# An RWKV-7 scan by quarters of its heads, its steps set between the products of the next quarter, and all late modulation sums on TensorE's column strips

## The chip, the cores and the metric

The kernel runs on one core of a Trainium2 chip. The metric is the time of one execution on the device in microseconds. Three runs of the kernel before gave 2135.18, 2140.97 and 2140.46 us; the median is 2140.46 us.

## The reference

Two blocks follow each other on one sequence of T = 256 tokens with D = 2048 channels, everything in float32. The change touches the first block's mixer and the modulation:

```python
mod = silu(c) @ ada_w + ada_b                  # six rows of 2048, from one vector c
sh_m, sc_m, g_m, sh_f, sc_f, g_f = split(mod + ada_table)
h = rms(x) * (1 + sc_m) + sh_m
r, k, v = (h + xx * mu[i]) @ w_rkv[i]          # each 2048 x 2048
# decay, a, g from low-rank products; kk = normalised k
def step(state, inp):                          # 32 heads of 64, over 256 tokens
    sa = state @ a_t
    state = state * w_t + sa b_t' + v_t k_t'
    return state, state @ r_t
y = groupnorm(y) * ln_w + ln_b + sum(r * k * r_k) * v
y = (y * g) @ w_o
x = x + g_m * rms(y)
h = rms(x) * (1 + sc_f) + sh_f
x = x + g_f * rms(conv_ffn(h))                 # then the second block
```

The scan is computed by chunks of 64 tokens. Inside a chunk of a head one 64x64 triangular system has to be inverted; from chunk to chunk the 64x64 state of the head is carried, so the four chunks of a head run in order, while heads are independent of each other.

## The kernel before

Every float32 weight tile of 128x1024 is read into a buffer "raw", split by ScalarE (ACT) into a high part "whi" (L142) and by VectorE (DVE) into the rest "wlo" (L146), and multiplied in three products on TensorE (PE): high by high, high by low, low by high. `fm_unit` (L149 to L159) does it with the tokens as the moving columns, 128x256 a product, 48 products for a weight tile pair of 2048 rows and 128 columns; `tm_units` (L161 to L192) does it with 512 weight columns moving. `split` (L133 to L147) is their common front.

The stages around the change are these, in time of the profiled execution. Until about 306 us the kernel makes the early modulation, v, k and the low-rank hidden layers. **The r stage**, about 306 to 467 us, is a loop over the 16 pairs of heads (L551 to L628): for each pair j it makes two low-rank products, the decay (L576 to L586, with tanh and exp on ACT), the r product (48 products of `fm_unit`) and the operands AR, BK and EC of the scan, which for all 16 pairs stay on the chip. The instruction at L605 is the first that reads the r product of a pair. **The scan**, 467 to 730 us, runs over all heads: `diag_gram` (L642) makes the products of 32x32 diagonal blocks, a mask and a transposition; `invert_diag` (L663) inverts 32 blocks at a time on 128 partitions in 30 dependent steps, each a product L680 and an addition L683 on DVE, in two column ranges (`PARTS`), and is run twice, for two chunks at a time; `gram`, `bt_make` and `invert_off` make the rest of the chunk's matrices. Then `chunk` (L746) runs four times. In it a group of 4 pairs goes through three steps: `stage_r` (products, then two copies to SBUF by ACT at L762), `stage_u` (products with these copies, two copies by ACT at L775), and `stage_o` (output and state products, state update on DVE at L801 to L804). The four groups of a chunk are independent and take turns, and `norm` (L824) of finished groups, the inversion for the later chunks, the gram products of the next chunk and the projection `e_proj` (L869) are set between them. **The w_o stage** follows from 698.7 us on in part and runs alone to 820.3 us; then the residual is added and the FFN's input made (the handover).

**The late modulation sums** are the twelve groups of 512 columns that the later rows g_m, sc_f and sh_f need. Before the change `ada_group` (L221 to L250) makes them on DVE: 16 row blocks of 128x512 for a group, each multiplied by a column of silu(c) and added to an accumulator (L239 for the first of a group, L245 for the others). One step of the generator is two reads of 512 KB and four blocks. The tables `RSKIP`, `ASTEP`, `OSTEP` and `LATE` set how many steps stand in the r stage, the scan, the w_o stage and the handover. The early sums use `ada_group_pe` instead (L252 to L268): four column strips of 32 columns of PE, block b on strip b mod 4, the weights as 512 moving columns (L263).

The program is written in this order, and the builder places each engine's instructions by its own estimate of when their inputs are ready, so that pieces of different loops stand between each other. Each engine then runs its own list in order. All reads and writes named here are issued by SyncE (SP), in the order of its list.

Of the kernel before, what the change touches and what calls it, by code (L numbers as in the profile page):

```python
# [8 lines left out]
F32 = mybir.dt.float32  # L9
# [7 lines left out]
NRAW, NRAW2 = 4, 5  # L17
NADA = 5
NADA2 = 3
NGL, NSTEP = 2, 2  # L20
HEAD = "d0 e v0 g0 b0 d1 g1 b1 e i0 e".split()
EPOS = ((0, 4),)
XL = 4
VST, WST, WP = (2, 2, 2, 2), (0, 0, 0, 0), 2
WLEAD = 5
EARLY = (("NT", 2), ("NT", 2), ("XT", 2), ("XT", 2))
# [4 lines left out]
A01 = (0, 1) * 6  # L31
ASTEP = (A01, A01, (0, 1, 1, 0, 1, 1, 0, 1, 1, 0, 1, 1), (1, 1, 1, 1, 1, 1, 0, 0))
OSTEP = (2, 2, 2, 0)
RSKIP = (0, 4)
# [31 lines left out]
def body(tc, A, out):  # L66
# [277 lines left out]
    sil32 = t_(pa, [P, KT, 32], "sil32")  # L344
# [42 lines left out]
    ada_how[0] = ada_group  # L387
# [95 lines left out]
    ada_how[0] = ada_group  # L483
# [47 lines left out]
    wide_m[0] = True  # L531
    pha.close()


    adx = ExitStack()
    adap[0] = adx.enter_context(pool("adap2", NADA2, side="right"))
    accp[0] = adx.enter_context(pool("accp", 2, side="right"))
    phb = ExitStack()
    pb = phb.enter_context(pool("pb", 1, side="right", reuse_waits="tile"))
    AR = t_(pb, [P, NPAIR, 4, P], "AR")  # L540
    BK = t_(pb, [P, NPAIR, 4, P], "BK")
    EC = t_(pb, [P, NPAIR, 4], "EC")
# [3 lines left out]
    bd = drm.tile([NPAIR, P, T], F32, tag="bd", name="bd")  # L546

# [6 lines left out]
    for j in range(NPAIR):  # L554
# [3 lines left out]
        l2h = t_(pr, [P, 4, P], "l2h", F32R, bufs=2)  # L558
        l2l = t_(pr, [P, 4, P], "l2l", F32R, bufs=2)
# [12 lines left out]
        for q, nm in ((0, "w"), (1, "a")):  # L572
            z = ps("m")
# [3 lines left out]
            th.append(t1)  # L577
        S.activation(th[0], th[0], AF.Copy, bias=1.0)
# [7 lines left out]
        S.activation(EC[:, j, :], c3(pc)[:, :, 63], AF.Exp, scale=C1)  # L586
# [5 lines left out]
        rb = ps("m")  # L592
# [3 lines left out]
        ar, bk = AR[:, j], BK[:, j]  # L596
# [12 lines left out]
        bb = ps("m")  # L609
# [6 lines left out]
        vT = t_(pr, [P, T], "vT", bufs=2)  # L616
        S.activation(vT, tp[:, :T], AF.Copy)
        V.tensor_tensor(vT, vT, bb[:, :T], op=ALU.mult)
        z = ps("s")
        low_rank(z[:, :T], [(2, "g0"), (3, "g1")])  # L620
        V.scalar_tensor_tensor(vT, vT, vcol(V_LNB, j), z[:, :T], op0=ALU.add, op1=ALU.mult)
        SP.dma_start(bd[j], vT)
        gs = t_(pr, [P, T], "gs", bufs=2)
        S.activation(gs, z[:, :T], AF.Copy, scale=vcol(V_LNW, j))
        SP.dma_start(gd[j], gs)
        if j % 8 not in RSKIP:
            next(ada, None)

    phr.close()
    whl_x.close()  # L630
    lora.close()


    phs = ExitStack()
    pc_ = phs.enter_context(pool("scan", 1, reuse_waits="tile"))
    ST = t_(pc_, [P, NPAIR, P], "ST")
    G.memset(ST, 0.0)
    yd = drm.tile([P, NPAIR, 2, 64], F32, tag="yd", name="yd")
    GT, UVs, NTs, XTs = {}, {}, {}, {}
    dmask = cst[:, DMK:DMK + 32]  # L640

    def diag_gram(w):  # L642

        a4 = t_(pc_, [P, 32, 32], "TQ")
        gp = [ps("s"), ps("s")]
        for e in range(2):
            for b in range(2):
                os_ = slice(e * 64 + b * 32, e * 64 + b * 32 + 32)
                bs = slice(b * 32, b * 32 + 32)
                for i in range(NPAIR):  # L650
                    for hd in range(2):
                        hs = slice(hd * 64, hd * 64 + 64)
                        mm(gp[hd][os_, i * 32:i * 32 + 32], BK[hs, i, 2 * w + e, bs], AR[hs, i, 2 * w + e, bs],
                           start=True, stop=True)
        ah = a4.rearrange("p (i h) t -> p i h t", h=2)
# [838 lines left out]
```

## Time and profile before

| | |
|---|---|
| median of three runs | 2140.46 us (2135.18 to 2140.97) |
| the profiled execution | 2133.21 us, span of the trace 2131.4 us |
| PE busy | 1979.3 us, 93% |
| DVE busy | 1385.3 us, 65% |
| ACT busy | 972.3 us, 46% |
| moved by DMA | 445.25 MB, mean 209 GB/s |

The profile is one execution. "Busy" counts an engine's instructions; matmuls are pipelined, so a matmul's own duration is longer than the interval to the next one. The granted clock is TensorE's, in tenths of full speed on the page and as a fraction in a window. An entry such as "idle 5.3 <-DVE wlo L146 5.3" says that the engine stood still for 5.3 us in all before this group of instructions, and that the end of a DVE instruction of line 146 on the tile wlo ended it.

### The profile page before, as it was taken

The page shows a single profiled execution, that of the slowest core. Times are in us where ns is not written, and L with a number is a line of the kernel's source. Part 1 is how long each engine was busy: PE and PEld are TensorE (multiplying, and loading weights), DVE is VectorE, ACT ScalarE, POOL GpSimd, SP SyncE. Part 2 cuts the span into 40 slices and gives each one's busy share as a digit, 9 for nine tenths or more (in the row PEclk, how much of TensorE's full clock was granted, in tenths as well). Part 3 has the DMA queues.
Part 4 walks back from the last instruction along what each step waited for, and adds up shares of the span by engine and source line. Part 5 has one row for each costly group of instructions (what it writes and reads, how often), then busy time and mean ns, then how long its engine had stood idle before and what let it go on. Part 6 is the DMA issues. An engine that isn't in the chain of part 4 may idle for free.

```text
span 2131.4 us, 36666 instructions
## 1 busy us (share of the span) xinstructions
PE 1979.3 (93%) x14708; PEld 1735.8 (81%) x14708; DVE 1385.3 (65%) x2203; ACT 972.3 (46%) x1514; POOL 386.8 (18%) x193
## 2 busy tenths in 40 slices
PE   6999989988878697899999999999989999999998
PEld 3688868886667486899999999788867899998887
DVE  3687899879778878966676766333353655656435
ACT  3544465533323244455545455344445444444453
POOL 1000000010000001323223232223232222222232
PEclk8999999998778798999999999999999999999999
DMA  8888668863667797866675766665645445456564
GB/s 279 309 273 299 208 223 293 259 182 108 151 159 214 233 324 256 278 224 191 194 251 190 213 202 196 217 192 188 195 153 170 134 166 164 159 163 208 184 201 148
DMA packets 189035, 445.25 MB, mean 209 GB/s; under 512 B 40120, under 2 KB 62776, under 8 KB 187328
## 3 DMA queue, kind: packets, MB, share of 16 engines
q1 hardware_dynamic: 188864, 442.91, 64.9%
q8 instruction: 115, 1.88, 0.4%
q14 instruction: 56, 0.46, 0.1%
HBM read 427.10 MB, written 15.75 MB: 208 GB/s over the span
## 4 chain that ended last, share of the span: by engine, by line
PE 63%; DVE 8%; DMA 6%; issue 1%; ACT 1%; SPq 0%; POOL 0%; DVEq 0%; ACTq 0%; POOLq 0%
PE ps_s L157 6%; PE ps_s L159 6%; PE ps_s L158 6%; PE ps_g L159 4%; PE ps_g L157 4%; PE ps_g L158 4%; PE ps_g L174 4%; PE ps_g L172 4%; DMA raw<-in_ada_w 4%; PE ps_g L173 4%; PE ps_s L172 4%; PE ps_s L174 4%; PE ps_s L173 4%; DVE acc L245 2%; DVE wlo L146 1%
## 5 line engine op out<-in xcount | busy, mean ns | idle before, releaser
L142 ACT ACTIVATE whi<-raw 128x1024 fp32r<-128x1024 f32 x558 | 590.1, 1059 | 665.6 <-PE ps_g L173 139.8
L146 DVE TENSOR_TENSOR wlo<-raw,whi 128x1024 fp32r<-128x1024 f32 x410 | 504.1, 1232 | 411.8 <-ACT whi L142 409.2
L146 POOL TENSOR_TENSOR wlo<-raw,whi 128x1024 fp32r<-128x1024 f32 x148 | 363.9, 2460 | 1085.7 <-ACT whi L142 1046.7
L159 PE MATMUL ps_g<-xh,wlo 128*128 128x256 f32 x816 | 233.8, 287 | 5.3 <-DVE wlo L146 5.3
L159 PE MATMUL ps_s<-xh,wlo 128*128 128x256 f32 x816 | 228.1, 279 | 7.3 <-DVE wlo L146 5.7
L157 PE MATMUL ps_g<-xh,whi 128*128 128x256 f32 x816 | 232.5, 285 | 0.5 <-ACT whi L142 0.5
L158 PE MATMUL ps_g<-xl,whi 128*128 128x256 f32 x816 | 231.4, 284 | 0.0
L157 PE MATMUL ps_s<-xh,whi 128*128 128x256 f32 x816 | 227.6, 279 | 0.0
L158 PE MATMUL ps_s<-xl,whi 128*128 128x256 f32 x816 | 227.4, 279 | 0.0
L245 DVE SCALAR_TENSOR_TENSOR acc<-raw,sil,acc 128x512 f32<-128x512 f32 x240 | 200.4, 836 | 35.3 <-DMA raw<-in_ada_w 33.6
L159 PEld LDWEIGHTS ps_g<-xh,wlo 128*128 128x128 f32 x816 | 158.0, 194 | 10.0 <-DVE wlo L146 7.5
L159 PEld LDWEIGHTS ps_s<-xh,wlo 128*128 128x128 f32 x816 | 155.0, 190 | 8.4 <-DVE wlo L146 6.5
L157 PEld LDWEIGHTS ps_g<-xh,whi 128*128 128x128 f32 x816 | 158.2, 194 | 2.7 <-issue 1.9
L158 PEld LDWEIGHTS ps_g<-xl,whi 128*128 128x128 f32 x816 | 158.0, 194 | 0.6 <-issue 0.3
L158 PEld LDWEIGHTS ps_s<-xl,whi 128*128 128x128 f32 x816 | 155.2, 190 | 0.0
L157 PEld LDWEIGHTS ps_s<-xh,whi 128*128 128x128 f32 x816 | 155.1, 190 | 0.0
L157 PE MATMUL ps_s<-h3h,whi 128*128 128x256 f32 x384 | 109.7, 286 | 0.0
L159 PE MATMUL ps_s<-h3h,wlo 128*128 128x256 f32 x384 | 108.4, 282 | 0.0
L158 PE MATMUL ps_s<-h3l,whi 128*128 128x256 f32 x384 | 108.2, 282 | 0.0
L582 POOL MEMSET ep<- 128x4 f32 x16 | 1.7, 107 | 437.9 <-DVE AR L605 225.1
L157 PEld LDWEIGHTS ps_s<-h3h,whi 128*128 128x128 f32 x384 | 72.4, 189 | 3.6 <-issue 3.5
L157 PE MATMUL ps_g<-h3h,whi 128*128 128x256 f32 x256 | 74.3, 290 | 0.0
(509 smaller groups left out, 4637.1 us busy)
## 6 DMA issues: line engine op xcount, KB each, us to landing
raw<-in_w_f SPq DMA_DIRECT2D x258, 512.0 KB, 4.6
raw<-in_ada_w SPq DMA_DIRECT2D x192, 512.0 KB, 5.3
raw<-in_w_i2f SPq DMA_DIRECT2D x80, 512.0 KB, 3.7
raw<-in_w_o SPq DMA_DIRECT2D x60, 512.0 KB, 5.1
raw<-in_w_v SPq DMA_DIRECT2D x32, 512.0 KB, 4.5
raw<-in_w_k SPq DMA_DIRECT2D x32, 512.0 KB, 5.1
raw<-in_w_r SPq DMA_DIRECT2D x32, 512.0 KB, 5.7
raw<-in_w_g SPq DMA_DIRECT2D x32, 512.0 KB, 4.8
```

The costliest lines, as they stand in the source:

```text
L142: S.activation(hi, raw, AF.Copy)
L146: e.tensor_sub(lo, raw, hi)
L157: mm(acc, wh[:, sl], xh[:, kt, :], start=(kt == 0), stop=False)
L158: mm(acc, wh[:, sl], xl[:, kt, :], start=False, stop=False)
L159: mm(acc, wl[:, sl], xh[:, kt, :], start=False, stop=(kt == KT - 1))
L172: mm(a, xh, wh[:, sl], start=st, stop=False)
L173: mm(a, xl, wh[:, sl], start=False, stop=False)
L174: mm(a, xh, wl[:, sl], start=False, stop=sp_)
L245: V.scalar_tensor_tensor(acc, raw[:, a, :], sc, acc, op0=ALU.mult, op1=ALU.add)
L582: G.memset(ep[:, :, 0:1], 1.0)
```

## The change

There are three parts.

First, the scan is cut by heads instead of by chunks alone. A quarter is 4 pairs, that is 8 heads. `scan(q)` does for a quarter all that was done for all heads: 32 diagonal blocks (8 heads by 4 chunks) on 64 partitions, one inversion of 30 steps, the gram products and transpositions between its steps, and four chunks whose three steps now have no other group beside them. The r stage of a pair has become the generator `operands`, with three points at which it hands over. At each of them, three steps of the scan of the quarter before are run (`SSTEP`). The scan of the last quarter has no later quarter: its steps stand beside the projection e, the reading back of the first three quarters' results from `yd`, and the first w_o products. Operands AR, BK and EC are held for two quarters instead of for all pairs.

Second, all late modulation sums use `ada_group_pe`, one step at each of the 48 hand-over points of the r stage (`QSTEP`); none stands in the w_o stage or the handover. The 192 instructions of L239 and L245 that they took on DVE go, 192 matmuls of 512 columns on strips come. The reads are the same, and there are three buffers for them (`NADA2`), as before.

Third, what this needs in space: two instead of three buffers for the split weights in the r stage (`NWHL`), one buffer for some operands that had two, and no early reading of w_o (`EARLY`, `WLEAD`).

The core of the diff:

```diff
-NRAW, NRAW2 = 4, 5
+NRAW, NRAW2, NWHL = 4, 5, 2
+SSTEP, QSTEP = 3, 1
-ASTEP = (A01, A01, (0, 1, 1, 0, 1, 1, 0, 1, 1, 0, 1, 1), (1, 1, 1, 1, 1, 1, 0, 0))
-OSTEP = (2, 2, 2, 0)
-RSKIP = (0, 4)
...
-    ada_how[0] = ada_group
     ada = ada_run(ADALAG, *[ada_row(2, k0, 4, V_NMP, gmd) for k0 in range(0, KT, 4)],
...
+    whl_x.close()
+    whl[0] = whl_x.enter_context(pool("whlr", NWHL, reuse_waits="tile"))
     adap[0] = adx.enter_context(pool("adap2", NADA2, side="right"))
...
-    for j in range(NPAIR):
+    def operands(j, AR, BK, EC):
...
         V.tensor_tensor(bk[:, :, 64:128], c3(k2), em, op=ALU.mult)
+        yield
         racc = ps("g")
         fm_unit(A["w_r"][j], xr, racc[:, :T])
+        yield
         rr = racc[:, :T]
...
         SP.dma_start(bd[j], vT)
-        if j % 8 not in RSKIP:
-            next(ada, None)
+        yield
...
+    def scan(q, AR, BK, EC):
         a4 = t_(pc_, [P, 32, 32], "TQ")
+        gp = [ps("m"), ps("m")]
+        for c in range(4):
             for b in range(2):
+                for i in range(4):
                     for hd in range(2):
+                        mm(gp[hd][bs, o:o + 32], BK[hs, i, c, bs], AR[hs, i, c, bs], start=True, stop=True)
+        ah = a4[0:64].rearrange("p (x h) t -> p x h t", h=2)
...
+        NT = t_(pc_, [P, 32, 32], "NT")[0:64]
+        V.transpose(NT, a4[0:64].rearrange("p u t -> p t u"))
+        yield
...
         for jj in range(30, 0, -1):
...
+            for c0, c1, n, pv in td:
+                V.tensor_tensor(pv, XT[:, c0:c1, jj:jj + 1].broadcast_to([64, n, jj]),
+                                NT[:, jj:jj + 1, 0:jj].broadcast_to([64, n, jj]), op=ALU.mult)
+            for c0, c1, n, pv in td:
                 V.tensor_tensor(XT[:, c0:c1, 0:jj], XT[:, c0:c1, 0:jj], pv, op=ALU.add)
+            if jj % 3 == 0:
+                next(sd, None)
+                yield
...
+        for c in range(4):
...
+            for hd in range(2):
                 S.activation(rs[:, hd, :], rp[hd * 64:hd * 64 + 64, 0:256], AF.Copy)
+            behind()
+            yield
             up = ps("s")
...
+            for hs in hss:
+                S.activation(uv[0:64, :, hs], up[hs, 0:256].rearrange("p (i d) -> p i d", d=64), AF.Copy)
+            behind()
+            yield
+            oy = ps("g" if q < 3 else "m")
...
+            S.activation(ys, oy[:, 256:].rearrange("p (i t) -> p i t", t=64), AF.Copy)
+            todo.append(norm(q, c, ys, gl, bl))
+            behind()
             yield
...
+    sc = iter(())
+    for q in range(4):
+        AR = t_(pb, [P, 4, 4, P], "AR")
+        BK = t_(pb, [P, 4, 4, P], "BK")
+        EC = t_(pb, [P, 4, 4], "EC")
+        for i in range(4):
+            for _ in operands(q * 4 + i, AR, BK, EC):
+                for _ in range(SSTEP):
+                    next(sc, None)
+                for _ in range(QSTEP):
+                    next(ada, None)
+        for _ in sc:
             pass
+        sc = scan(q, AR, BK, EC)
+    for _ in ada:
+        pass
...
+    for e, _ in enumerate(sc):
+        if e % 3 == 0:
+            nb = next(ep_, None)
+            if nb is not None:
+                e_proj(nb, pT)
+        elif e % 3 == 1:
+            q = next(yq, None)
+            if q is not None:
...
+                SP.dma_start(yt, yd[:, q4, :])
+                for hf in range(2):
+                    y_split(yh[hf][:, :, q4, :], yt[:, :, hf * P:hf * P + P])
...
-                 [(nb, kt, kt == 0, kt == KT - 1) for kt in range(KT)], lead=WLEAD if nb == 0 else 0, more=more, tail=TAIL if nb == 3 else 0,
-                 early=early if nb == 0 else ())
+                 [(nb, kt, kt == 0, kt == KT - 1) for kt in range(KT)], tail=TAIL if nb == 3 else 0)
...
-        for _ in range(OSTEP[nb]):
-            next(ada, None)
```

The order of PE in a chunk. Before, the products of one chunk step (L755 is `stage_r`, L772 `stage_u`, L786 and L788 `stage_o`) stand beside those of another group and the projection e (L869):

```order
L869 MATMUL ps_g<-raw,ys 128x512 x2
L755 MATMUL ps_s<-uv,xh 64x64
L772 MATMUL ps_s<-rs,xh 64x64 x8
L869 MATMUL ps_g<-raw,ys 128x512 x2
L786 MATMUL ps_g<-uv,BK 64x64 x2
L788 MATMUL ps_g<-xh,uv 64x64 x2
```

After, L150 to L152 are the three r products of the next quarter (L157 to L159 before), L613 is another product of the r stage, L784, L797 and L808 to L813 are the steps r, u and o of a chunk, and L665 is a norm's last product:

```order
L152 MATMUL ps_g<-xh,wlo 128x256
L150 MATMUL ps_g<-xh,whi 128x256
L151 MATMUL ps_g<-xl,whi 128x256
L152 MATMUL ps_g<-xh,wlo 128x256
L797 MATMUL ps_s<-rs,GT 64x64 x8
L665 MATMUL ps_m<-rx,selc 128x256
L784 MATMUL ps_s<-uv,GT 64x64 x2
L613 MATMUL ps_s<-qb,cst 128x256
L808 MATMUL ps_g<-uv,BK 64x64 x2
L810 MATMUL ps_g<-GT,uv 64x64 x2
L813 MATMUL ps_g<-AR,ST 64x64 x2
L808 MATMUL ps_g<-uv,BK 64x64 x2
```

Between two steps of one quarter's chunk there now stand products of the next quarter's r stage and a norm, and no other group of heads.

The order of PE in the r product. Before, it is a plain run of three alternating products, with low-rank products (L567 to L569) between:

```order
L569 MATMUL ps_a<-lhiw,l2l 128x256
L159 MATMUL ps_g<-xh,wlo 128x256
L157 MATMUL ps_g<-xh,whi 128x256
L158 MATMUL ps_g<-xl,whi 128x256
L159 MATMUL ps_g<-xh,wlo 128x256
```

After, matmuls on strips (L256, which was L263) stand between them, in groups of changing length:

```order
L594 MATMUL ps_s<-rk_146,selc 128x256
L256 MATMUL ps_a<-raw,sil_102 32x512 x2
L150 MATMUL ps_g<-xh,whi 128x256
L151 MATMUL ps_g<-xl,whi 128x256
L256 MATMUL ps_a<-raw,sil_102 32x512 x10
L152 MATMUL ps_g<-xh,wlo 128x256
L150 MATMUL ps_g<-xh,whi 128x256
```

In the r stage after the change there are 70 such groups with 192 matmuls: 18 groups of one, 26 of two, 5 of three, 11 of four, 5 of five, 3 of six and 2 of ten.

The order of ACT around the norm's square root. Before, one table load (at L336) stands at the first norm, and the copies of the chunks (L762, L775) need none:

```order
L762 ACTIVATE rs<-ps_s 64x256 x2
L793 ACTIVATE ys<-ps_g 128x256
L775 ACTIVATE uv<-ps_s 64x4x64 x2
L835 ACTIVATE rt<-ps_m 128x256
L336 ACT_TABLE_LOAD
L336 ACTIVATE rn<-ps_m,epsr 8x64
L871 ACTIVATE gl<-ps_g 128x512
L762 ACTIVATE rs<-ps_s 64x256
```

After, L655 is the norm's square, L329 its square root, and L586 an exponential of the r stage:

```order
L575 ACTIVATE zs<-ps_s 128x256
L584 ACTIVATE ep<-pc 128x4x64
L577 ACTIVATE gs<-zs,vec 128x256
L329 ACT_TABLE_LOAD
L329 ACTIVATE rn<-ps_m,epsr 8x64
L586 ACT_TABLE_LOAD
L586 ACTIVATE em<-pc 128x256
L587 ACTIVATE EC<-pc 128x4
```

The square roots of the norms and the exponentials and tanhs of the r stage now alternate on ACT: the whole program has 25 table loads after the change and 11 before, and 13 of the 25 lie in the r stage with the scans beside it and in the last scan.

## Rows read from the trace of the kernel before

**Rows 1.** The page: granted TensorE clock in tenths, and GB/s, in 40 slices.
```profile
PEclk8999999998778798999999999999999999999999
...
GB/s 279 309 273 299 208 223 293 259 182 108 151 159 214 233 324 256 278 224 191 194 251 190 213 202 196 217 192 188 195 153 170 134 166 164 159 163 208 184 201 148
```

**Rows 2.** Windows by stage: length, engines' busy time (instructions), granted clock, DMA share, GB/s.
```profile
306.00:318.00 12.00, 11.34 (x81) 10.46 (x81) 11.37 (x17) 8.03 (x16) 0.00 (x0) 0.93 0.84 286
318.00:467.00 149.00, 140.18 (x1031) 128.94 (x1030) 135.12 (x259) 82.91 (x176) 3.91 (x17) 0.94 0.80 248
467.00:730.00 263.00, 205.36 (x2929) 162.28 (x2922) 206.57 (x514) 78.26 (x182) 6.96 (x6) 0.77 0.65 175
730.00:821.00 91.00, 90.03 (x388) 73.54 (x388) 70.81 (x87) 35.63 (x46) 1.74 (x1) 0.98 0.84 296
821.00:846.00 25.00, 10.19 (x70) 9.50 (x71) 21.03 (x38) 13.78 (x34) 6.38 (x3) 0.66 0.60 222
```

**Rows 3.** One source line (L605, the r product's first reader), with first and last start.
```profile
L605 DVE TENSOR_TENSOR AR<-ps_g,ep x16: 413/424/426, 318.1 to 466.5; 128x256 f32<-128x256 f32 x16
```

**Rows 4.** Timeline of PE in a weight tile's products: start, duration, operation.
```profile
437.52 0.28 PE L159 MATMUL ps_g<-xh,wlo 128*128 128x256 f32 x1
...
440.40 0.28 PE L159 MATMUL ps_g<-xh,wlo 128*128 128x256 f32 x1
```

**Rows 5.** Timeline of PE around sums on strips (L263), two records a matmul.
```profile
39.94 1.06 PE L263 MATMUL ps_a<-raw,sil 128*32 128x512 f32 x8
...
43.92 1.05 PE L263 MATMUL ps_a<-raw,sil 128*32 128x512 f32 x2
...
44.90 0.50 PE L425 MATMUL ps_s<-wlo,xl 128*128 128x512 f32 x1
...
154.01 1.92 PE L263 MATMUL ps_a<-raw,sil 128*32 128x512 f32 x16
```

**Rows 6.** Lines of DVE, 306 to 822 us: instructions, busy us, mean ns, idle before.
```profile
L245 DVE SCALAR_TENSOR_TENSOR acc<-raw,sil,acc 128x512 f32<-128x512 f32 x180 | 135.0, 751 | 26.1 <-DMA raw<-in_ada_w 24.9
...
L680 DVE TENSOR_TENSOR pt<-XT,NT 128x108 f32<-128x108 f32 (+33 forms) x106 | 22.6, 247 | 0.1
...
L683 DVE TENSOR_TENSOR XT<-XT,pt 128x108 f32<-128x108 f32 (+33 forms) x106 | 22.4, 246 | 0.1
...
L723 DVE STREAM_TRANSPOSE TQ<-XT 32x1024 f32<-32x1024 f32 x4 | 7.9, 1966 | 0.0
...
L803 DVE TENSOR_TENSOR ST<-ST,ps_g 64x256 f32<-64x256 f32 x16 | 6.6, 415 | 0.3
```

**Rows 7.** Lines of ACT, 306 to 822 us.
```profile
L775 ACT ACTIVATE uv<-ps_s 64x256 f32<-64x256 f32 x32 | 12.1, 379 | 6.8 <-PE ps_s L772 6.4
...
L762 ACT ACTIVATE rs<-ps_s 64x256 f32<-64x256 f32 x32 | 12.1, 379 | 20.3 <-PE ps_s L759 15.6 <-remote 3.2 <-PE ps_s L755 0.5
...
L336 ACT ACT_TABLE_LOAD x1 | 1.3, 1283 | 0.0
```

**Rows 8.** Timeline of ACT around a table load.
```profile
312.65 1.28 ACT L576 ACT_TABLE_LOAD   x1
313.95 0.48 ACT L576 ACTIVATE thw<-ps_m,dv 128x256 f32<-128x256 f32 x1
```

**Rows 9.** Lines of PE, 460 to 730 us.
```profile
L869 PE MATMUL ps_g<-raw,ys 128*128 128x512 f32 x32 | 20.3, 794 | 0.0
```

**Rows 10.** One source line (L172, w_o's first product), with first and last start.
```profile
L172 PE MATMUL ps_g<-whi,xh x32: 392/392/628, 698.7 to 795.2; 128*128 128x512 f32 x32
...
L172 PE MATMUL ps_s<-whi,xl x32: 388/390/392, 754.7 to 819.5; 128*128 128x512 f32 x32
```

**Rows 11.** Timeline of DVE at the handover.
```profile
818.90 0.75 DVE L245 SCALAR_TENSOR_TENSOR acc<-raw,sil,acc 128x512 f32<-128x512 f32 x1 [0.73 <-DMA raw<-in_ada_w]
...
819.69 2.74 DVE L245 SCALAR_TENSOR_TENSOR acc<-raw,sil,acc 128x512 f32<-128x512 f32 x1
```

**Rows 12.** The page: DMA issues, KB each, us to landing.
```profile
raw<-in_ada_w SPq DMA_DIRECT2D x192, 512.0 KB, 5.3
```

More of the change, by code (lines that the diff above doesn't have):

```diff
@@ new lines, in scan, with uv_load, side @@
+        yield
+        Gt = t_(pc_, [P, 32, P], "GT")
+        g4 = Gt.rearrange("p (c i h) t -> p c i h t", i=4, h=2)
+        def uv_load(c):
+            uv = t_(pc_, [P, 4, P], "uv", bufs=2)
+            SP.dma_start(uv[64:128].rearrange("p i d -> p (i d)"),
+                         vd[c // 2, (c % 2) * 64:(c % 2) * 64 + 64, q * 512:(q + 1) * 512])
+            G.memset(uv[0:64], 0.0)
+            return uv
+        def side():
+            for c in range(4):
+                gram(g4, c, AR, BK)
+                yield
+            for c in range(3):
+                bt_make(c, BK)
+                yield
@@ L743, in invert_off, with behind @@
         yield
-    def chunk(c, ys):
-        Gt, uv = GT[c], UVs[c]
-        def stage_r(i4):
+        ST = t_(pc_, [P, 4, P], "ST")
+        G.memset(ST, 0.0)
+        todo = []
+        def behind():
+            while todo:
+                try:
+                    next(todo[0])
+                    return
+                except StopIteration:
+                    todo.pop(0)
+        hss = [slice(hd * 64, hd * 64 + 64) for hd in range(2)]
+        for c in range(4):
+            un = uv_load(c + 1) if c < 3 else None
+            cs = slice(c * 64, c * 64 + 64)
+            gl = t_(pc_, [P, 4, 64], "gl", bufs=2)
+            SP.dma_start(gl, gd.rearrange("j p t -> p j t")[:, q * 4:q * 4 + 4, cs])
+            bl = t_(pc_, [P, 4, 64], "bl", bufs=2)
+            SP.dma_start(bl, bd.rearrange("j p t -> p j t")[:, q * 4:q * 4 + 4, cs])
@@ L766, in stage_u @@
+            yield
             up = ps("s")
             for i in range(4):
[L768 removed]
                 o = slice(i * 64, i * 64 + 64)
[L770 to L775 removed]
@@ L873, in e_proj @@
             S.activation(ev[:, 512:1024], ev[:, 0:512], AF.Square, accum_out=esq[:, hf, nb:nb + 1])
-    def run(*gs):
-        for _ in chain(*gs):
-            pass
-    EP = iter(range(4))
-    def dgg(w):
-        diag_gram(w)
-        yield
-    def epg():
-        nb = next(EP, None)
-        if nb is not None:
-            e_proj(nb)
-        yield
-    HD = {"d0": lambda: dgg(0), "d1": lambda: dgg(1), "v0": lambda: invert_diag(0, PARTS), "i0": lambda: invert_off(0),
-          "i1": lambda: invert_off(1),
-          "g0": lambda: gram(0), "g1": lambda: gram(1), "b0": lambda: bt_make(0), "b1": lambda: bt_make(1), "e": epg}
@@ L1047, in body @@
     accs = tm_accs()
-    wx = ExitStack()
-    more = wx.enter_context(pool("wx", WLEAD - 3, side="right", reuse_waits="tile")) if WLEAD > 3 else None
     for nb in range(4):
```

357 lines of the change are left out of this document (115 added, 242 removed).

## The prediction

> **What bounds the kernel now.** I read the page's clock and GB/s lines first, to see where the engines are not fed [rows 1]: from the tenth to the fourteenth slice the clock digits are 7 and 8 and the DMA moves 108 to 233 GB/s, while the fifteenth, in w_o, reaches 324. The windows by stage give the reason for each stage [rows 2]. In the r stage PE is busy 140.18 of 149 us and DVE 135.12: both are nearly full, at a granted clock of 0.94. In the scan PE has 205.36 and DVE 206.57 of 263 us, at a clock of 0.77: neither is full, they wait for each other, and PE works slower because of it. The w_o stage is PE alone, 90.03 of 91 us at 0.98. At the handover DVE is busy 21.03 of 25 us. One pair of heads takes (466.5 - 318.1)/15 = 9.9 us in the r stage [rows 3]; its 48 r products have an interval of (440.40 - 437.52)/24 = 0.12 us, so 5.8 us of it [rows 4]. From 306 us to the end of w_o's last product at about 820.3 us (the last L172 starts at 819.5 [rows 10] and two products follow) it is 514 us, and this stretch is what the change rebuilds. DVE is busy in it for 135.12 + 206.57 + 70.81 = 412 us, of which 135.0 are the late sums [rows 6]: 180 instructions of 751 ns.
>
> **The change, part by part.** I add up the new stretch as four pieces, all against the profiled execution.
>
> A. The first quarter has no scan beside it. Each pair now reads 1 MB of w_r, about 0.77 MB of small operands and stored rows, and three steps of two reads of 512 KB for the late sums, together 4.98 MB (before, 12 steps stood over 16 pairs). The fastest slice of the trace moves 324 GB/s, the r stage 248 and w_o 296 [rows 1, 2]. At 324 a pair takes 15.4 us, at 296 16.8, where it took 9.9. Since some of the sums' data is read ahead I take 15, that is 60 us for four pairs, and the 12 us from 306 to the first L605 as before: 72. Bounds: 66 (reads well ahead) and 80 (at 296 and an SP list that stands behind a full buffer). PE's work, 37 + 18 us by the figures of B, lies under it.
>
> B. Three quarters with a scan beside them. For each:
> r products and operands: PE is busy 140.18/149 of the 9.9 us, 9.3 us a pair, 37 us. DVE's relief does not lower this, since PE is nearly full there already.
> Sums on strips: four matmuls on four strips take 1.06 us, one alone takes the same (1.05, and PE's next product starts 0.98 after it), eight take 1.92 [rows 5]. So a group costs about 0.96 us for each four or part of four. The 70 groups of the order are 82 such turns, 79 us in all, about 20 us a quarter. Bounds: at the rate of eight, 0.24 a matmul, 48 of them are 11.5 us; each alone at 0.98 is 47. The order decides for the middle.
> Scan on PE: 205.36 less the 20.3 of projection e [rows 9] is 185 us at a clock of 0.77. At 0.98 this would be 145, so 36 to 46 a quarter; I take 37, since r products keep PE busier than the scan alone did.
> Hand-overs: before, four groups of a chunk took turns, and an ACT copy of one lay beside another's products. Now a quarter has one group, and its steps r, u and o follow each other through two pairs of ACT copies of 379 ns [rows 7] and four state updates of 415 ns on DVE [rows 6]: 4 x 0.379 + 4 x 0.415 = 3.2 us a chunk, 12.7 for four. r products stand between them in the order, but not after every step. Between 0 (all covered) and 12.7 I take 8.
> Table loads: 13 of 1.283 us [rows 7, 8] lie in this stretch, four a quarter, 5 us of ACT; ACT is busy 82.91 of 149 us in the r stage, so most of it is hidden. Bounds 0 and 5, I take 2.
> In the trace the activation after such a load starts 0.02 us after its end [rows 8], so a load costs its 1.283 us and nothing more. The Trainium skill (ScalarE: Activation LUTs, section What ACT_TABLE_LOAD costs) adds a drain of about 1380 ns for every switch, 2.66 us; by that rule, four would be 11 us of ACT a quarter and, with the same share hidden, the sum would be 2 us a quarter higher. The trace doesn't show the drain.
> Together 37 + 20 + 37 + 8 + 2 = 104 a quarter, 312 for three. DVE has 135 us less to do, but 32 blocks on 64 partitions are inverted four times instead of twice: L680 and L683 take 22.6 + 22.4 = 45 us for two [rows 6], so 22.5 for each quarter and 45 more in all. That leaves DVE at 412 - 135 + 45 = 322 us of the new stretch: not the bound, except while an inversion runs. By a rule of the Trainium skill (TensorEngine Tiling (Array Packing), section Key Properties), a change of the tiling mode drains TensorE; the strips force two for every group. Beside it the trace has PE's next product 0.98 us after a single strip matmul [rows 5], which is in my price already.
>
> C. The scan of the last quarter alone. It is a chain, and only projection e (20.3 us, rows 9) and the first w_o products fill it: inversion 22.5; transpositions of 1.97 us [rows 6], four of them, 8; four chunks at 3.2 us of copies and updates plus three runs of small products and their hand-overs, estimated 8.5 each, 34; the diagonal products, gram masks, off blocks, last norm and split have no row in which they lie alone, estimated 30 (15 to 45). Sum 95, from 80 to 110.
>
> D. What is left of w_o. Of 384 products the order has 133 beside the last scan, 251 behind it, at 90.03/388 = 0.232 us [rows 2]: 58.
>
> 72 + 312 + 95 + 58 = 537 against 514: 23 us later. At the handover, DVE's late sums go, the last of which run from 819.69 for 2.74 us, past PE's end [rows 11]: 3 back. The FFN's four groups stay as they are. So 20 us longer: 2133.2 becomes 2153, and as the profiled execution lies 7.3 us under the median, the forecast is 2160 us.
>
> **The rivals.**
> First, faster: the products cover every hand-over, and PE keeps the upper of its two levels (1.2 and 2.4 GHz) through the scans, as in w_o (0.98), where the old scan had 0.77 [rows 2]. Then a quarter is 35 of r stage, 14 of strips, 36 of scan, 3 of the rest, 88; A 70, C 88 and D 58: 480, which is 34 less, and 3 at the handover: 2103. For it speaks that PE waits for DVE in the old scan and that 135 us of DVE work go; against it that the strips put new work on PE, which is the fuller engine in the r stage and in w_o. It decides as soon as a quarter takes less than about 97.
> Second, slower still: the strips stand in PE's list ahead of r products, and their data comes through three buffers, each landing 5.3 us after its issue [rows 12]. A group of ten matmuls needs five reads, two more than there are buffers. If each of a quarter's 12 steps of two reads waits 0.8 us, a quarter is 10 us longer: three make 30, 2190. Old L245 waited so, 26.1 us for 180 [rows 6], but there DVE stood, not PE.
> Third, no change: the hand-overs are covered, but the strips are not cheaper: 98 a quarter, C 90, sum 514, 2140.
>
> **How the numbers follow.** I give 0.43 to the forecast, 0.28 to the first rival, 0.17 to the second and 0.12 to the third. A measurement of this kernel can tell 0.3%, 6.4 us, from no change. The third case is the middle of "same", and the edges of its neighbours reach into it: faster 0.31, same 0.14, slower 0.55. With A from 66 to 80, C from 80 to 110 and a quarter between 96 and 112, the likeliest case's own range is 2140 to 2180; the whole one reaches to 2095, past the first rival, and up to 2198, past the second.
>
> **What would show it.** In the profile after: the windows of the first quarter's four pairs with DMA above 300 GB/s and 15 us a pair (A); 104 us between the first r products of successive quarters, the clock above 0.9, and PE idle behind the ACT copies rs and uv (B); groups of strips at about 1 us for up to four matmuls; a stretch of some 95 us with PE half idle ahead of the bulk of w_o (C). If the quarters with a scan take 90 us and PE shows no gaps there, the first rival is right and my strips and hand-overs are overpriced. If PE's waits are for the reads of ada_w, it is the second. If the first quarter takes 40 us, A fails, and the time is 20 us lower.

## The result, and the profile after

The change made the kernel slower: 2211.24 us in the median of four runs (2202.98 to 2219.71) against 2140.72, a ratio of 1.0334 with a 95% interval of 1.0286 to 1.0382, some 71 us. The forecast was 20 us slower, so the sign was right, the size was not, and 2211 lies above the range.

The page after has these two lines, the granted clock in tenths and the GB/s of 40 slices, which answer to [rows 1]:

```profile
PEclk8999998889999989899999999999999999999999
...
GB/s 291 297 297 283 206 199 205 200 200 217 197 209 152 207 150 303 212 193 180 185 183 248 181 213 190 175 233 193 191 196 135 177 144 175 170 165 219 191 197 153
```

The clock no longer falls to 7 in the old scan's slices, and the DMA moves about 200 GB/s where the r stage had 248. The windows after, in order: three pairs of the first quarter, the three quarters with a scan beside them, the start and the rest of the last scan, the bare w_o, the handover. Each quarter ends at the first reader of its last r product (L608, which was L605). The columns are those of [rows 2]: length, busy time of PE, PEld, DVE, ACT and POOL with instructions, granted clock, DMA share, GB/s.

```profile
323.20:384.00 60.80, 44.99 (x288) 30.33 (x287) 22.96 (x46) 18.54 (x40) 0.32 (x3) 0.89 0.72 223
384.00:511.40 127.40, 104.60 (x1094) 73.18 (x1098) 76.38 (x212) 47.62 (x97) 3.56 (x11) 0.88 0.76 203
511.40:620.90 109.50, 104.76 (x1104) 71.80 (x1100) 75.69 (x214) 45.56 (x95) 3.13 (x10) 0.97 0.66 202
620.90:730.10 109.20, 104.43 (x1104) 71.03 (x1100) 75.19 (x212) 43.78 (x92) 3.13 (x10) 0.97 0.58 177
730.10:770.30 40.20, 31.32 (x273) 16.40 (x268) 27.78 (x100) 16.34 (x32) 0.15 (x1) 0.96 0.77 220
770.30:831.00 60.70, 55.75 (x608) 40.82 (x608) 37.95 (x80) 25.49 (x50) 1.04 (x2) 0.89 0.47 145
831.00:899.30 68.30, 66.65 (x290) 53.68 (x288) 50.52 (x61) 29.10 (x38) 1.46 (x1) 1.00 0.90 313
899.30:925.00 25.70, 10.05 (x63) 9.24 (x63) 23.27 (x41) 16.33 (x39) 6.63 (x3) 0.67 0.61 209
```

Against the terms of the sum: A was 72 us and is 384.0 - 306 = 78. B was 104 a quarter and is 127.4, 109.5 and 109.2, together 346 instead of 312. C was 95 and is 101. D was 58 and is 68.3, since 98 products of w_o were run beside the last scan, not 133. Together 593 us, where the sum had 537: the stretch ends at 899.4 us instead of 820.3, 79 later. What follows this stretch took 1302 us in this execution against 1311 before; in the runs below it took 1306 to 1320, so the 9 us are taken as the scatter of one execution and not as the change's.

In A the DMA moved 223 GB/s over the last three pairs, not above 300. These pairs took 14.3, 30.9 and 15.6 us. In the long one, a read of w_r stands in the chain that ended last (start, us, what); over the whole program such a read landed 7.3 us after its issue in the median, and 5.7 before:

```profile
345.38 13.48 DMA raw<-in_w_r
```

The first reader of the r product, with its first and last start, stretches over 407 us instead of 148 [rows 3]:

```profile
L608 DVE TENSOR_TENSOR AR<-ps_g,ep x16: 411/424/425, 323.2 to 730.1; 128x256 f32<-128x256 f32 x16
```

The strips by themselves, PE's busy time on L256 in the first two quarters with a scan, some 48 matmuls of two records each:

```profile
384.00:511.40 127.40, 23.82 (x100) 3.25 (x104) 0.88 0.76 203
511.40:620.90 109.50, 25.84 (x100) 3.75 (x96) 0.97 0.66 202
```

Their price of 20 us was 24 to 26. What PE waited for in the same two quarters (total us, times, longest):

```profile
PE ps_a L256 <- DMA raw<-in_ada_w: 15.3, 3, 9.0
...
PE ps_a L256 <- DMA raw<-in_ada_w: 2.4, 3, 1.6
```

So in the first of them PE stands 15.3 us for reads of the late sums, and in the second hardly at all; there PE is busy 104.76 of 109.5 us at a clock of 0.97. The chain that ended last, within each of the two quarters by lines (the view ends the row where it does), says the same: 21.7% and 4.0% of it are these reads.

```profile
by line: DMA raw<-in_ada_w 21.7%; PE ps_a L256 13.4%; PE ps_g L152 7.7%; PE ps_g L150 7.4%; PE ps_g L151 7.1%; another core or an unknown queue 3.6%; PE ps_m L636 2.4%; PE ps_s L561 1.9%; DVE wlo L139 1.9%; PE ps_m L653 1.9%; PE ps_m L665 1
...
by line: PE ps_a L256 18.4%; PE ps_g L151 5.9%; PE ps_g L150 5.7%; PE ps_g L152 5.4%; PE ps_m L636 5.2%; DMA raw<-in_ada_w 4.0%; PE ps_s L561 3.3%; PE ps_g L808 2.8%; PE ps_m L665 2.8%; PE ps_m L273 2.5%; PE ps_g L810 2.4%; PE ps_s L613 2.3
```

Read alone, the second quarter says that PE is the bound and the strips are the loss. The experiments show that this is not all of it.

DVE's inversion, which answers to L680 and L683 of [rows 6], doubled as forecast, to 89.5 us:

```profile
L729 DVE TENSOR_TENSOR XT<-XT,pt 64x140 f32<-64x140 f32 (+28 forms) x212 | 44.8, 243 | 0.1
L726 DVE TENSOR_TENSOR pt<-XT,NT 64x140 f32<-64x140 f32 (+29 forms) x212 | 44.7, 242 | 0.1
```

The table loads cost what [rows 8] had, with the next activation 0.02 us behind:

```profile
505.27 1.28 ACT L586 ACT_TABLE_LOAD   x1
506.57 0.42 ACT L586 ACTIVATE em<-pc 128x256 f32<-128x256 f32 x1
```

At the handover nothing was won, against the 3 us of the forecast: PE waits 14.65 us for its first product (14.49 before), and the first sums of the FFN's own groups (L238) now stand where the others went.

```profile
897.37 3.54 DVE L238 SCALAR_TENSOR_TENSOR acc<-raw,sil,acc 128x512 f32<-128x512 f32 x2 [1.28 <-DMA raw<-in_ada_w]
...
914.09 0.48 PE L933 MATMUL ps_a<-cst,y 128*128 128x128 f32 x1 [14.65 <-DVE y L929]
```

### The profile page after: what moved, and what is told of

Read it like the earlier page. It is cut to its first block, busy times and chain, and to the rows that moved or that the text cites. A ratio compares the mean times of both kernels' runs of the same rounds, so it can differ in the third digit from the quotient of the medians.

```text
span 2201.2 us, 37566 instructions
## 1 busy us (share of the span) xinstructions
PE 2054.0 (93%) x15092; PEld 1728.1 (79%) x15092; DVE 1312.3 (60%) x2229; ACT 1001.7 (46%) x1554; POOL 387.7 (18%) x210
## 4 chain that ended last, share of the span: by engine, by line
PE 81%; DMA 8%; DVE 6%; ACT 3%; issue 1%; SPq 0%; another core or an unknown queue 0%; POOL 0%; ACTq 0%; DVEq 0%; POOLq 0%
PE ps_s L150 6%; PE ps_s L152 6%; PE ps_s L151 6%; PE ps_g L150 5%; PE ps_g L152 5%; PE ps_g L151 5%; PE ps_a L256 4%; DMA raw<-in_ada_w 4%; PE ps_s L165 4%; PE ps_g L167 4%; PE ps_s L166 4%; PE ps_s L167 4%; PE ps_g L166 4%; PE ps_g L165 4%; DVE wlo L139 1%; PE ps_s L438 1%
## 5 line engine op out<-in xcount | busy, mean ns | idle before, releaser
L139 DVE TENSOR_TENSOR wlo<-raw,whi 128x1024 fp32r<-128x1024 f32 x414 | 509.7, 1233 | 457.0 <-ACT whi L135 454.2
L150 PE MATMUL ps_g<-xh,whi 128*128 128x256 f32 x816 | 236.8, 290 | 14.7 <-ACT whi L135 14.7
L152 PE MATMUL ps_g<-xh,wlo 128*128 128x256 f32 x816 | 236.8, 290 | 3.0 <-DVE wlo L139 2.9
L151 PE MATMUL ps_g<-xl,whi 128*128 128x256 f32 x816 | 236.0, 289 | 0.0
L152 PE MATMUL ps_s<-xh,wlo 128*128 128x256 f32 x816 | 231.1, 283 | 2.7 <-DVE wlo L139 2.7
L150 PE MATMUL ps_s<-xh,whi 128*128 128x256 f32 x816 | 231.1, 283 | 0.0
L150 PEld LDWEIGHTS ps_g<-xh,whi 128*128 128x128 f32 x816 | 160.5, 197 | 26.3 <-ACT whi L135 16.7
L256 PE MATMUL ps_a<-raw,sil 128*32 128x512 f32 (+1 forms) x704 | 139.7, 591 | 36.5 <-DMA raw<-in_ada_w 26.6
L152 PEld LDWEIGHTS ps_g<-xh,wlo 128*128 128x128 f32 x816 | 160.2, 196 | 13.0 <-issue 6.2
L152 PEld LDWEIGHTS ps_s<-xh,wlo 128*128 128x128 f32 x816 | 156.6, 192 | 3.1 <-DVE wlo L139 3.1
L150 PEld LDWEIGHTS ps_s<-xh,whi 128*128 128x128 f32 x816 | 156.8, 192 | 0.0
L150 PE MATMUL ps_s<-h3h,whi 128*128 128x256 f32 x384 | 107.8, 281 | 0.0
L152 PE MATMUL ps_s<-h3h,wlo 128*128 128x256 f32 x384 | 106.6, 278 | 0.0
L256 PEld LDWEIGHTS ps_a<-raw,sil 128*32 128x32 f32 x704 | 23.3, 110 | 82.2 <-DMA raw<-in_ada_w 41.1
L150 PEld LDWEIGHTS ps_s<-h3h,whi 128*128 128x128 f32 x384 | 72.2, 188 | 3.6 <-issue 3.5
L152 PEld LDWEIGHTS ps_s<-h3h,wlo 128*128 128x128 f32 x384 | 72.3, 188 | 0.3 <-issue 0.3
```

Of the source, the lines that this page charges most:

```text
L139: e.tensor_sub(lo, raw, hi)
L150: mm(acc, wh[:, sl], xh[:, kt, :], start=(kt == 0), stop=False)
L151: mm(acc, wh[:, sl], xl[:, kt, :], start=False, stop=False)
L152: mm(acc, wl[:, sl], xh[:, kt, :], start=False, stop=(kt == KT - 1))
L256: mm(acc[r:r + 32, :w_], sil32[:, b, :], raw[:, a, :], start=(b < 4), stop=(b >= KT - 4))
```

## The experiments

Each is compared with the kernel before, run on the same chip in turns; the ratio is what counts. The changed kernel itself has 1.0334. The letters of the theories are those of the expectations and not the terms A to D of the sum.

**The strips without their time.**

```diff
-                mm(acc[r:r + 32, :w_], sil32[:, b, :], raw[:, a, :], start=...
+                cw = 32 if seg >= 2 else w_
+                mm(acc[r:r + 32, :cw], sil32[:, b, :], raw[:, a, :cw], start=...
```

Expected: 

> The changed kernel, but each late strip matmul moves 32 of its 512 columns (the rest of the late sums is left out); all reads of 512 KB stay. Theory A, the strips' time on TensorE is the loss: the strips go from 98 us of PE to under 15, a quarter with a scan beside it from 109 to about 88 us, the first quarter stays at its reads, the whole is 2125 to 2150 us. Theory B, the reads behind three buffers are the loss: nothing but the matmul goes, the time stays above 2190. Theory C, the cut of the scan itself is the loss (twice the inversions, one group a chunk): also above 2180, with PE waiting for DVE and ACT instead.

Measured: 1.0252 (1.0207 to 1.0298), 2204.64 us. The window of the second quarter with a scan:

```profile
505.60:609.70 104.10, 90.88 (x1105) 76.48 (x1102) 75.95 (x215) 46.06 (x94) 3.56 (x11) 0.87 0.75 227
```

The quarter went from 109.5 to 104.1 us only, with PE now at a clock of 0.87 where it had 0.97; the quarters beside it took 122.4 and 109.9 us (127.4 and 109.2 in the changed kernel). Theory A fell: the strips' time alone is not what a quarter lasts. The first quarter, with all its reads, stayed at 77.2 us.

**The sums back on DVE, in the new places.**

```diff
+    ada_how[0] = ada_group
     ada = ada_run(ADALAG, *[ada_row(2, ...
...
-        kr = t_(pr, [P, T], "kr", bufs=2)
+        kr = t_(pr, [P, T], "kr")                # and so for vl
```

Expected: 

> The changed kernel with the late sums back on DVE at the same 48 places (two one-buffer tiles in the r stage pay for the accumulators). DVE then has 75 + 36 = 111 us of work in a quarter of 109, PE 82. Theory A: a quarter stays at about 105 to 112 us, now bound by DVE, the whole 2185 to 2220. Theory C (the cut is the loss whoever makes the sums): the same, but if the quarters become 95 or less, the strips alone were the loss, and the time is below 2160.

Measured: 1.0429 (1.0375 to 1.0482). The same quarter:

```profile
522.10:640.30 118.20, 91.33 (x1016) 78.02 (x1012) 104.38 (x262) 46.10 (x93) 3.12 (x10) 0.78 0.62 188
```

118 us with DVE busy 104.38: with the sums there DVE is the fuller engine, as expected, and the quarter is longer than expected. What the two tiles with one buffer cost in it is not shown.

**Groups of 256 columns.**

```diff
-    ada = ada_run(ADALAG, *[ada_row(2, k0, 4, V_NMP, gmd) for k0 in range(0, KT, 4)],
+    ada = ada_run(ADALAG, *[ada_row(2, k0, 2, V_NMP, gmd) for k0 in range(0, KT, 2)],
...                                              # and so for sc_f, sh_f
```

Expected: 

> The changed kernel with late groups of 256 columns instead of 512: a read of 512 KB then brings four blocks, one for each strip, so that four matmuls become ready at once; 384 matmuls of half the length. In the order these are 114 turns of up to four, half as long, where there were 82. Theory A: strips 98 us before, about 60 to 70 now, the time 2170 to 2190. Theory B: the reads have rows of 1 KB instead of 2 KB, no gain, 2205 or more.

Measured: 1.0473 (1.0434 to 1.0513), worse than the change. PE's waits in the first quarter with a scan:

```profile
PE ps_a L256 <- DMA raw<-in_ada_w: 25.1, 6, 8.3
```

The strips took less time on PE (18.4 us of busy in the next quarter instead of 25.8), and the waits for reads rose from 15.3 to 25.1 us. So the reads were part of the loss.

**The kernel before without most of its sums' time.**

```diff
-                    V.scalar_tensor_tensor(acc, raw[:, a, :], sc, acc, ...
+                    cw = 32 if seg < 5 else w_
+                    V.scalar_tensor_tensor(acc[:, :cw], raw[:, a, :cw], sc, acc[:, :cw], ...
```

Expected: 

> The kernel before, but each late sum on DVE after a group's first takes 32 of its 512 columns (the rest is left out), reads as before. It shows what the late sums cost there, and beside the run of the changed kernel with 32 columns what the cut of the scan alone does. Theory A: DVE loses some 110 us of the 514, half of it on the path in the scan; 2090 to 2120, so that the cut alone is no gain either, or a loss of up to 30 us. If it stays at 2135 or above, the late sums were free before, and the whole loss is the strips.

Measured: 0.9805 (0.9763 to 0.9848), 42 us less. The stretch that answers to the 263 us of the scan in [rows 2], 219.6 us, and the sums as they are now (L246, which was L245):

```profile
458.20:677.80 219.60, 195.49 (x2956) 158.20 (x2954) 154.33 (x483) 77.28 (x181) 7.46 (x6) 0.80 0.67 174
...
L246 DVE SCALAR_TENSOR_TENSOR acc<-raw,sil,acc 128x32 f32<-128x32 f32 x174 | 42.7, 245 | 21.3 <-DMA raw<-in_ada_w 19.4
```

The late sums were not free before. An instruction of 32 columns still takes 245 ns, so only some 92 of the 135.0 us [rows 6] are gone, and they give back some 42 us. What the rest would give no run shows.

**Reads issued by POOL; stores issued by POOL.** Two runs, the first with the late sums' reads, the second with the stores moved that the r stage writes for the norms (gd, bd) and the scans write for w_o (yd):

```diff
-            SP.dma_start(raw, A["ada_w"][...
+            (G if seg >= 2 else SP).dma_start(raw, A["ada_w"][...
```

```diff
-        SP.dma_start(gd[j], gs)
+        G.dma_start(gd[j], gs)                   # and so for bd and yd
```

Expected of the first: 

> The changed kernel with the late sums' reads issued by POOL instead of SP, all else as it is. With the strips' time taken away the quarters stayed at 104 to 122 us, so the reads pace them too. Theory D, SP's list holds them up (a read waits behind stores whose data comes late, and w_r's reads wait behind a late-sum read whose buffer is not free): the second quarter loses its 18 us above the others, the time is 2180 to 2195. Theory E, the transfers themselves are the pace (DMA share 0.76 at 203 GB/s with many short rows): 2205 to 2220.

Expected of the second: 

> The changed kernel with the stores of gd, bd and yd issued by POOL instead of SP, so that reads don't stand behind stores that wait for their data. Theory D: 2180 to 2200. Theory E: 2205 to 2220.

Measured: 1.0539 (1.0465 to 1.0614) and 1.0302 (1.0228 to 1.0376). The first was worse than the change, the second the same within its interval: that reads stand behind these stores in SP's list is not what holds the quarters. For the place of the late reads themselves the first run is no clean test, since the reads came later: in the first quarter with a scan those by POOL landed 6.0 us after their issue in the median, where by SP it was 5.2, and those of w_r 10.8 instead of 7.9. PE's waits in that quarter, reads by POOL:

```profile
PE ps_a L256 <- DMA raw<-in_ada_w: 32.5, 8, 10.1
```

**A quarter of the sums.**

```diff
+        kt = 4 if seg >= 2 else KT
-        for q in range(KT // n):
+        for q in range(kt // n):
...
-    ada = ada_run(ADALAG, *[ada_row(2, ...
+    ada = ada_run(0, *[ada_row(2, ...           # a row is finished at once, not two steps later
...
+                n_y[0] += 1
+                if n_y[0] % 4 == 0:
+                    next(ada, None)
```

Expected: 

> The changed kernel with only the first 4 of the 16 row blocks of each late group read and summed on strips, one step at every fourth place (three quarters of the late sums are left out). Both the strips' time and their reads go. If these two together are the loss: first quarter 45 to 50 instead of 78 us, the others 84 to 88, the whole 2085 to 2110. Theory C, the cut of the scan is a loss by itself: above 2130.

Measured: 1.0115 (1.0044 to 1.0186), 2173.91 us. The first quarter and the three with a scan:

```profile
306.00:354.90 48.90, 41.92 (x287) 35.03 (x286) 33.70 (x60) 31.43 (x60) 0.83 (x5) 0.90 0.78 235
354.90:479.60 124.70, 104.51 (x1031) 84.33 (x1030) 75.31 (x212) 46.19 (x95) 3.12 (x10) 0.74 0.49 119
479.60:588.90 109.30, 95.71 (x1030) 78.28 (x1030) 75.57 (x215) 46.17 (x95) 3.12 (x10) 0.81 0.40 120
588.90:698.00 109.10, 95.66 (x1029) 78.23 (x1029) 74.90 (x212) 44.41 (x92) 3.12 (x10) 0.81 0.30 88
```

The first quarter falls to 49 us, and with the strips short but all the reads it had stayed at 77.2: term A of the sum was the reads. The others stay at 124.7, 109.3 and 109.1 us, with a quarter of the strips and the DMA at 88 to 120 GB/s. So neither strips nor reads alone make a quarter's length. Even so the kernel is slower, clear of its interval, than the one before with all its sums.

**A third of the sums in the last scan.** 

```diff
+                n_y[0] += 1
+                if n_y[0] % 3:
                     next(ada, None)
...
     for e, _ in enumerate(sc):
+        if e >= 2:
+            next(ada, None)
```

Expected: 

> The changed kernel with two of three hand-over points taking a late-sum step in the r stage, and the other 16 steps in the last scan, where the DMA moves 145 to 220 GB/s and PE idles some 18 us. The quarters lose a third of their strips (8 us of 25) and of their reads: first quarter 62 instead of 78, the others 100 and 112 instead of 109 and 127; the last scan gets 16 strips' turns of 1 to 2 us, some 15 us longer. 2165 to 2190. If the quarters stay as they are, neither reads nor strips pace them.

Measured: 1.0403 (1.034 to 1.0466). The first quarter took 71 us, the quarters with a scan 106, 117 and 101, and the last scan to the end of w_o 229 instead of 169: what was moved cost more there.

**A third of the inversion.** To the kernel with a quarter of the sums:

```diff
-            for c0, c1, n, pv in td:
+            for c0, c1, n, pv in td if jj % 3 == 0 else ():
```

Expected: 

> The changed kernel with a quarter of the late sums (as the run before this one that had it, 2174 us) and with 10 of the 30 steps of each inversion (the other 20 are left out): 15 us less of DVE a quarter. Theory G, the quarter with a scan beside it is paced by the scan's own chain, in which the inversion stands whole: the quarters fall from 109 to about 94, the last scan too, the whole 2105 to 2125. Theory H, PE's products at the lower clock are the pace: the quarters stay above 105, the whole above 2150.

Measured: 0.9887 (0.9851 to 0.9923), 49 us less than with the whole inversion. The quarters with a scan:

```profile
349.40:467.40 118.00, 105.03 (x1031) 84.68 (x1030) 63.38 (x140) 45.94 (x95) 3.12 (x10) 0.75 0.51 130
467.40:559.00 91.60, 87.35 (x1031) 71.86 (x1030) 63.48 (x142) 45.53 (x95) 3.13 (x10) 0.93 0.47 139
559.00:655.00 96.00, 91.76 (x1030) 75.14 (x1029) 62.83 (x140) 43.81 (x92) 3.12 (x10) 0.88 0.34 101
```

DVE lost 12 us a quarter, and the quarters 7, 18 and 13, together as much as DVE. With a quarter of the sums the inversion stands in the path: theory G. With all the strips this was not run.

**No steps between the products.** With a quarter of the sums:

```diff
-SSTEP, QSTEP = 3, 1
+SSTEP, QSTEP = 0, 1
```

Expected: 

> The changed kernel with a quarter of the late sums and no scan step at the hand-over points (SSTEP 0): a quarter's scan is written whole behind the next quarter's operands. It prices the chain alone: with 40 us for four pairs and 95 for a scan by itself a quarter is 135 instead of 109, the whole 2174 + 3 x 26 = 2250. If it is 2200 or less, the steps between the products gained little, and the scan's chain alone is about as long as the quarter with both.

Measured: 1.0378 (1.0352 to 1.0405). The scan of the first quarter with one pair beside it, and the three pairs after it:

```profile
408.70:505.00 96.30, 69.80 (x810) 54.15 (x810) 52.33 (x167) 26.53 (x54) 2.79 (x7) 0.70 0.30 94
505.00:537.50 32.50, 32.10 (x222) 26.91 (x221) 24.15 (x48) 19.39 (x42) 0.32 (x3) 0.95 0.67 202
```

A scan with one pair takes 96.3 us, a pair 32.5/3 = 10.8, so a scan alone is estimated at 85 us, if nothing of the pair is hidden; the next scan with a pair took 90.3. PE is busy 69.8 of the 96.3 us and DVE 52.33: neither is full, they wait for each other. In the same window PE's longest wait is for the inversion's end:

```profile
PE ps_m L750 <- DVE TQ L740: 17.1, 1, 17.1
```

**All the strips, a quarter of the reads.** With a quarter of the reads, each of their blocks multiplied four times:

```diff
-            for a in range(n):
+            for a in list(range(n)) * (4 if seg >= 2 else 1):
```

Expected: 

> The changed kernel with a quarter of the late reads, but every block of them multiplied four times: all 192 strip matmuls, a quarter of the reads (the sums are not those of the reference). Theory G: the strips lie in the chain's waits and hold the clock up, so the quarters stay at 109 to 113 and the whole at 2174 to 2190; what the full kernel has above that is the reads. If the strips are on the path: 25 us more a quarter at the same clock, 2230 and more.

Measured: 1.0169 (1.0137 to 1.02), 2185.3 us:

```profile
306.00:360.10 54.10, 49.12 (x323) 35.76 (x324) 32.20 (x57) 29.03 (x57) 0.76 (x4) 0.94 0.81 219
360.10:468.00 107.90, 101.80 (x1103) 75.90 (x1103) 74.76 (x213) 45.86 (x95) 3.12 (x10) 0.92 0.56 127
468.00:580.50 112.50, 106.08 (x1102) 78.93 (x1102) 75.74 (x215) 45.80 (x95) 3.12 (x10) 0.88 0.41 117
580.50:692.80 112.30, 106.29 (x1101) 79.04 (x1100) 75.08 (x212) 43.96 (x92) 3.12 (x10) 0.88 0.30 86
```

Against a quarter of both, the strips add 0.0054, some 12 us, which is within the two intervals; against the changed kernel, the rest of the reads is 0.0165, some 35 us, most of it in the first two quarters (54.1 and 107.9 us here against 78 and 127.4). The two are not cleanly parted: the 192 matmuls stand in fuller groups here and took 75.5 us of PE instead of 98.2. A second way has the strips short in both runs: 1.0252 with all the reads less 1.0115 with a quarter of them, 29 us for the reads, and 18 for the strips.

**Six steps instead of three.** With a quarter of the sums:

```diff
-SSTEP, QSTEP = 3, 1
+SSTEP, QSTEP = 6, 1
```

Expected: 

> The changed kernel with a quarter of the late sums and six scan steps instead of three at each hand-over point, so that a quarter's scan stands beside two pairs instead of four. If the quarter is the scan's chain plus what of the r stage is not hidden in it, closer packing leaves two pairs of 10 us bare: the quarters go from 109 to 110 to 118, the whole 2175 to 2200. If the spacing by three steps itself stretched the chain: quarters below 104, the whole below 2160.

Measured: 1.022 (1.0175 to 1.0265). A scan with two pairs, then two pairs:

```profile
482.30:569.20 86.90, 65.56 (x812) 54.09 (x808) 57.18 (x174) 27.34 (x60) 1.92 (x6) 0.78 0.36 108
569.20:598.40 29.20, 28.89 (x223) 22.32 (x224) 18.52 (x41) 18.34 (x36) 1.20 (x4) 0.94 0.55 176
```

A scan with two pairs takes 86.9 us, about what the run without steps has for it alone; two pairs hide, the other two are bare with 29.2. Spread by threes, the four pairs add 109.3 - 85 = 24 us to a scan. Close packing is no better, and the spacing is not what stretches the chain.

**Strips in the old scan.** Three runs of the kernel before: six late groups on strips instead of DVE, the same in groups of 256 columns, and three of the six in groups of 256.

```diff
+        ada_how[0] = ada_group_pe if 3 <= u < 9 else ada_group
```

Expected: 

> The kernel before, its scan not cut, with the six late groups that stand in the scan (groups 3 to 8 of 12) on strips instead of DVE, and two psum banks instead of three in rotation there; the other six stay on DVE. It is the second part of the change alone, in the stage where PE idles 58 of 263 us at a clock of 0.77. If the loss is the cut of the scan and not the strips: DVE loses 72 us there, PE gains some 50 us which partly fill its idle time and hold the clock up; the scan 235 to 255 us instead of 263, the whole 2115 to 2140. If strips are the loss: 2160 or more.

> The kernel before with the six late groups of the scan on strips as in the run that made no change, but in groups of 256 columns, so that one read brings four blocks and the four strips run together: in the order 54 turns of half the length instead of 51 whole ones, some 30 us of PE instead of 50. If the strips' partly filled turns took back what DVE's 72 us gave, the scan falls from 263 to 240 to 250 us and the whole is 2120 to 2135. If the scan is paced by its own chain or by the reads: 2145 and more.

> The same with every second of these six groups on strips and the others on DVE: 36 us less of DVE and 15 us more of PE in the scan. If the two engines hand over in turns, the balance is what counts: 2120 to 2135, not behind the run with all six. If it is the reads: 2145 and more.

Measured: 0.9982 (0.9951 to 1.0013), 1.0015 (0.9992 to 1.0038) and 0.9984 (0.996 to 1.0008): no change in any. The scan of the first:

```profile
467.00:730.00 263.00, 238.62 (x3123) 153.96 (x3121) 149.68 (x416) 81.53 (x188) 7.46 (x6) 0.92 0.65 169
```

DVE lost 57 us and PE gained 33 at a clock of 0.92 instead of 0.77 [rows 2]; the stage stays as long. Neither filled strips nor a balance of the two engines gave a gain, so both explanations of it fell. All three also had two psum banks instead of three in rotation there; what this costs is not shown. None of the versions with all of the work beats the kernel before.

## Why the prediction was wrong

The forecast stretch was 537 us and the measured one is 56 longer: 6 in A, 23 in the first quarter with a scan, 11 in the other two together, 6 in C, 10 in D.

The step that failed is "Together 37 + 20 + 37 + 8 + 2 = 104 a quarter, 312 for three": it puts the reads of the late sums at nothing, and the three quarters took 346. The prediction had these reads only in its second rival, at 10 us in every quarter. They came in one: in the first quarter with a scan PE waits 15.3 us for them and the chain runs through them for 21.7% of 127.4 us; with a quarter of the reads and all the strip matmuls this quarter took 107.9. In all, the reads that were left out cost 29 to 35 us, by the two ways above. Without them the time would be an estimated 2176 to 2182 us (2211 less 35 or 29), inside the stated range.

In the other two quarters 104 lies near 109.5 and 109.2, and its terms can be read: PE is busy 104.76 us where its three terms had 94 (strips 25.84 instead of 20, all else 79 instead of 74), and idle 4.7 where hand-overs and table loads had 10. But PE's list is not the only thing of that length. Without most of the strips the quarters last as long, 109.3 us, and PE, less busy, runs at 0.81 instead of 0.97. What holds them then is the scan's chain through DVE, PE and ACT, an estimated 80 to 87 us by itself, as the runs without steps between and with six steps show, in which the inversion's 22.5 us stand, as the run with a third of it shows; and of the 43 us of four pairs only some 14 to 19 are hidden in it (96.3 + 32.5 = 128.8 us apart, or 122.9 the next time, 109.3 together). The sum for these quarters has no term for this chain. The prediction had it in hand as C, 95 us, and used it for the last quarter only, although the same chain runs in every quarter. So two limits of nearly one length lie side by side, the agreement of 104 with 109 is in part luck, and taking away the strips alone wins little. Whether the chain alone would win anything with all the strips in place no run shows. The 37 us for the scan, a fourth of the old scan's work on PE, hides this: the old chain carried four groups of pairs in turns, 219.6 us for all heads with most of the sums' time gone; the new one carries one group and is walked four times.

A's 78 lies within its bounds, and the reads make it: with a quarter of them it was 49 to 54. But it was to come from a rate above 300 GB/s at 15 us a pair, and the DMA moved 223, with one pair of 30.9 us that stood for a read of w_r; that the number came out near is in part luck. C's 101 was within its bounds. D's 10 us were my count of the products beside the last scan, 133 where 98 ran, taken from the order, which says what can stand beside and not what is ready. The table loads and the doubled inversion were sized right, and the loads did not show in PE's waits.

By ratios, in steps from the kernel before to the changed one: most of the sums' time off DVE gives back 0.0195, 42 us; from there to the cut scan with a quarter of the sums it costs 1.0115 - 0.9805, 66 us; then the strips 12 and the reads 35. These steps add up to 71 by the way they are taken, so the sum is no proof of them. The 66 us are the least exact, since the two kernels left out different parts of the sums, and they hold the third part of the change too (two buffers for the split weights, one for some operands, no early reading of w_o), which no run tried by itself.

What stays open is why the first quarter with a scan took 124.7 us where the next took 109.3 even with a quarter of strips and reads; with all strips and few reads it did not (107.9). The trace shows where it went: PE stood 8.5 us amid the first scan's diagonal products (L688) for nothing that the profile shows, and was busy 8.8 us longer, at a granted clock of 0.74 instead of 0.81. With all strips and few reads there is no such wait, at a clock of 0.92.

```profile
PE ps_m L688 <- issue: 8.5, 2, 5.7
```

## What to carry to other kernels

Before a dependent chain is cut into more, narrower pieces, price one piece alone: a quarter of the members did not make a quarter of the chain, some 85 us instead of 219.6 for all heads, so four quarters in a row cost more than the whole. A stretch in which one engine is 96% busy may have a chain of the same length beside it: take that engine's work away before counting on the gain. Give every read that moves into a stretch a term of its own there. And the order of a list shows what may run beside what, not what will be ready.

## What the runs showed of the hardware

With work taken off TensorE the granted clock went down and the time stayed: with 25.84 us of strips in a quarter the clock was 0.97 and the quarter 109.5 us, with a quarter of the strips and reads 0.81 and 109.3 us. In groups of 256 columns, whose reads of 512 KB have rows of 1 KB instead of 2 KB, PE waited 25.1 us for them in a quarter instead of 15.3, though the strips took less. With the reads issued by POOL, the same bytes, it waited 32.5 us.
